# Gate and value projections of a gated MLP as seven half-width products per pair of chunks

## The chip, the cores and the metric

One NeuronCore of a Trainium2 chip runs the whole program in one launch. The metric is device time in microseconds of that launch. Three runs of the kernel before gave 1490.82 us as their median (1489.89 to 1491.82). A separate profiled execution took 1491.45 us; all rows of the trace shown here come from that one execution.

## The reference

A decoder trunk of two layers on 512 tokens of 1024 channels, in float32. Each layer has a token mixer (layer 0: a gated linear recurrence with pooling; layer 1: a Conformer convolution module), a cross-attention into 256 memory tokens, and a gated MLP. Only the MLP matters here:

```python
D_MODEL = 1024; SEQ = 512; D_FF = 3 * D_MODEL; CONV_F = 3

def conv_ffn(x, norm, w_up, dw_w, dw_b, w_down):
    h = rms_norm(x, norm) @ w_up                       # 1024 -> 6144
    g = causal_dwconv(h[..., :D_FF], dw_w, dw_b)       # gate half, 3 taps over tokens
    u = h[..., D_FF:]                                  # value half
    return (jax.nn.gelu(g) * u) @ w_down               # 3072 -> 1024

def reference(...):
    for layer in range(2):
        x = x + (mixer_ab if layer == 0 else conformer_conv)(...)
        x = x + cross_attn(x, mem, ...)
        x = x + conv_ffn(x, f_norm[layer], f_w_up[layer], ...)
    return rms_norm(x, final_norm)
```

## The kernel before

Activations lie with channels on the 128 partitions and the 512 tokens in the free dimension: `X[c]`, c from 0 to 7, each 128x512. A weight comes from HBM as a 128x1024 piece (512 KB) into a `raw` tile on the SP queue (`load_w`, L147). To keep float32 accuracy with the faster fp32r matmul, every operand is split in two: a high half, rounded by ACT (L161), and a low half, the difference, by DVE or, where told so, Pool (L162). `mm3` (L167 to L169) then makes three matmuls for each 128x128 weight block: high x high, high x low, low x high, all accumulated in one PSUM bank.

The MLP's 3072 gate and 3072 value channels are 24 chunks of 128 each. `up(c)` makes one gate chunk (eight weight blocks against eight activation tiles, 24 matmuls of 512 columns) and one value chunk. The activations it reads, `norm.x`, are X times the norm's gain, split but not yet divided by the root mean square; that scale, `norm.r`, is multiplied into the gate chunk on its way out of PSUM (L474) and into the result by Pool (L481). Between them stand the three taps (ACT L477, DVE L479 twice), the gelu (ACT L480), and the product with the value chunk out of PSUM (L483); the result is split into `ys[c]`. After every four chunks but the first four, `down(g)` multiplies the results of the group before with the down weights, eight products of 12 matmuls, each added to X by DVE (L494). The last group's down product goes together with the squares for the next norm (`nxt.feed`), or in layer 1 with the final norm (`finish`).

In layer 0 the memory tokens for layer 1's attention (`Memory(1)`) are loaded before the MLP and scaled and split (`mem.operand`, L312 and L313) in its second group. Four key weight pieces are split ahead ("parked") before the last down product.

A scheduler sets the order of instructions on each engine from dependencies and priorities: within `tc.high_priority(n)` instructions are drawn ahead. Tiles come from pools with a fixed number of buffers; a tile waits until a buffer is free. PSUM has five banks for products (`main_ps`), two further ones (`aux_ps`) and one for statistics.

Of the kernel before, what the change touches and what calls it, by code (L numbers as in the profile page):

```python
# [10 lines left out]
F32 = mybir.dt.float32  # L11
# [4 lines left out]
P = 128  # L16
# [12 lines left out]
AHEAD = 100  # L29
URGENT = 600  # L30
# [27 lines left out]
def trunk(ctx: ExitStack, tc: tile.TileContext, I: dict, out: list):  # L58
# [83 lines left out]
    def load_w(src=None, eng=None, raw=None, parts=1, ahead=AHEAD, park=False):  # L142

        with tc.high_priority(0 if raw is not None else ahead):
# [107 lines left out]
    def scale_of(ps, n=T, keep=False):  # L252
        sd = tmp_f(n)
        A.activation(sd, ps[:, :n], AF.Sqrt, bias=eps)
        r = small.tile([P, n], F32, tag="rs" if keep else "r", name=nm("r"), bufs=1 if keep else 2)
        V.reciprocal(r, sd)
        return r
# [209 lines left out]
    def ffn(layer, norm, nxt, mem=None):  # L467
        ys = {}

        def up(c):  # L470
            ps = project(load_w(I["wup"][(layer * 2) * CF + c]), c, norm.x)
            g = tmp_f(T + 2)
            G.memset(g[:, :2], 0.0)  # L473
            V.tensor_tensor(g[:, 2:], ps, norm.r, op=ALU.mult)  # L474
            y = tmp_f()
            dw = lambda j: col("f_dw_w", (layer * 3 + j) * CF + c)
            A.activation(y, g[:, 2:], AF.Identity, scale=dw(2), bias=col("f_dw_b", layer * CF + c))  # L477
            for j in (1, 0):
                V.scalar_tensor_tensor(y, g[:, j : j + T], dw(j), y, op0=ALU.mult, op1=ALU.add)  # L479
            A.activation(y, y, AF.Gelu_apprx_tanh)  # L480
            G.tensor_tensor(y, y, norm.r, op=ALU.mult)  # L481
            ps = project(load_w(I["wup"][(layer * 2 + 1) * CF + c]), c, norm.x)
            V.tensor_tensor(y, ps, y, op=ALU.mult)  # L483
            ys[c] = split(y)

        def down(g):
            for j in range(C // 2):
                w = load_w(I["wdown"][(layer * NG + g) * (C // 2) + j])
                for i in range(2):
                    n = 2 * j + i  # L490
                    ps = mm_ps()
                    for k in range(GC):
                        mm3(ps, blk(w, k * 2 * P + i * P), ys[g * GC + k], k == 0, k == GC - 1)
                    V.tensor_tensor(X[n], X[n], ps, op=ALU.add)  # L494
                    if g == NG - 1:
                        nxt.feed(n)

        for g in range(NG):
            for c in range(g * GC, (g + 1) * GC):
                up(c)  # L500
            if g:
# [533 lines left out]
```

## Time and profile before

| | |
|---|---|
| median of three runs | 1490.82 us |
| profiled execution | 1491.45 us |
| its span | 1489.6 us |
| MLP of layer 0 | about 365 to 757 us in the span |
| MLP of layer 1 | from about 1092 us to the end |
| DMA | 156.76 MB, 105 GB/s in the mean |

The columns of the views are these. In the list of groups: line, engine, operation, tile written <- tiles read, shapes, count, then total busy us and mean ns of one, then idle time of that engine just before them and what ended it. In a timeline: start us, duration us, engine, line, operation; "x4" behind it means four in a row merged into one entry. In the table of windows: stretch, its length, busy us (and count) of PE, PEld, DVE, ACT and POOL, granted clock, DMA share, GB/s. PE is the matmul engine, PEld its weight loads; `mm` and `aux` are PSUM tiles, `whi`, `wlo` and `act` split operands, `tmp` 128x512 work tiles, `bigr` 128x1024 split operands. Matmuls are pipelined: one lists 0.28 or 0.39 us, but the next starts earlier.

### The profile page before, as it was taken

To read this page: it belongs to the slowest core of one execution; us is meant where nothing else is said; L and a number is where in the kernel's file an instruction comes from. 1 tells how busy PE (TensorE), PEld (TensorE's weight loads), DVE (VectorE), ACT (ScalarE), POOL (GpSimd) and SP (SyncE) were. 2 spreads that over 40 slices of the span, in tenths; PEclk is the share of its full clock that TensorE was granted. 3 is DMA by queue.
4 is the path that set the end of the run, shared out by engine and by line. 5 is a ranking of instruction groups with operands and counts; after the bars stand their busy time and mean duration, and the time that the engine had idled before them with its cause. 6 is when DMAs were issued, how large, how long until landed. Compare 5 with 4: busy or idle time off the path is not lost.

```text
span 1489.6 us, 17802 instructions
## 1 busy us (share of the span) xinstructions
PE 1471.9 (99%) x6948; PEld 1211.3 (81%) x6948; DVE 912.9 (61%) x1220; ACT 638.3 (43%) x894; POOL 202.1 (14%) x228
## 2 busy tenths in 40 slices
PE   8999999999999999999999999999999999999997
PEld 7988788888888888888887666888888888888887
DVE  7877774647655545455666996666565554555455
ACT  7568743435432323323435346544443332323333
POOL 0012300000110101001006862300001010101001
PEclk9999999999999999999999999999999999999999
DMA  7522343213333333333416553321223333333321
GB/s 277 158 88 97 114 127 94 68 37 114 99 99 97 90 96 99 100 99 97 149 52 176 163 147 127 110 85 57 77 94 99 99 99 100 90 96 97 99 85 57
DMA packets 46820, 156.76 MB, mean 105 GB/s; under 512 B 5264, under 2 KB 6288, under 8 KB 46736
## 3 DMA queue, kind: packets, MB, share of 16 engines
q1 hardware_dynamic: 46448, 155.36, 33.6%
q8 instruction: 54, 0.88, 0.2%
q10 hardware_dynamic: 288, 0.27, 0.1%
q14 instruction: 30, 0.25, 0.0%
HBM read 145.13 MB, written 2.10 MB: 99 GB/s over the span
## 4 chain that ended last, share of the span: by engine, by line
PE 85%; issue 3%; DVE 2%; POOL 2%; ACT 1%; DMA 0%; POOLq 0%; DVEq 0%; ACTq 0%
PE mm L167 27%; PE mm L168 27%; PE mm L169 26%; PE aux L169 1%; PE aux L168 1%; PE aux L167 1%; PE aux L809 1%; POOL tmp L664 1%; DVE wlo L162 1%; POOL act L162 0%; PE aux L417 0%; DVE big L640 0%; ACT whi L161 0%; DMA raw<-in_wv 0%; DVE act L162 0%
## 5 line engine op out<-in xcount | busy, mean ns | idle before, releaser
L169 PE MATMUL mm<-act,wlo 128*128 128x512 f32 (+1 forms) x1797 | 697.5, 388 | 2.5 <-DVE wlo L162 2.5
L167 PE MATMUL mm<-act,whi 128*128 128x512 f32 (+1 forms) x1797 | 698.5, 389 | 0.0
L168 PE MATMUL mm<-act,whi 128*128 128x512 f32 (+1 forms) x1797 | 697.6, 388 | 0.4 <-DVE act L162 0.4
L161 ACT ACTIVATE whi<-raw 128x1024 fp32r<-128x1024 f32 x259 | 274.0, 1060 | 575.1 <-PE mm L168 477.4
L167 PEld LDWEIGHTS mm<-act,whi 128*128 128x128 f32 x1797 | 337.3, 188 | 73.9 <-issue 3.3
L169 PEld LDWEIGHTS mm<-act,wlo 128*128 128x128 f32 x1797 | 337.3, 188 | 72.0 <-DVE wlo L162 3.3
L168 PEld LDWEIGHTS mm<-act,whi 128*128 128x128 f32 x1797 | 337.4, 188 | 69.7 <-DVE act L162 1.3
L162 DVE TENSOR_TENSOR wlo<-raw,whi 128x1024 fp32r<-128x1024 f32 x239 | 296.5, 1242 | 65.3 <-ACT whi L161 62.5
L481 POOL TENSOR_TENSOR tmp<-tmp,r 128x512 f32<-128x512 f32 x48 | 62.0, 1292 | 637.5 <-ACT tmp L480 632.6
L494 DVE TENSOR_TENSOR x<-x,mm 128x512 f32<-128x512 f32 x88 | 60.4, 687 | 97.0 <-PE mm L169 97.0
L474 DVE TENSOR_TENSOR tmp<-mm,r 128x512 f32<-128x512 f32 x48 | 33.2, 692 | 125.7 <-PE mm L169 125.6
L483 DVE TENSOR_TENSOR tmp<-mm,tmp 128x512 f32<-128x512 f32 x48 | 33.2, 691 | 95.5 <-POOL tmp L473 87.2
L834 DVE SCALAR_TENSOR_TENSOR aux<-h,par,aux 128x491 f32<-128x491 f32 (+16 forms) x106 | 71.9, 726 | 2.1 <-PE aux L809 1.1
L479 DVE SCALAR_TENSOR_TENSOR tmp<-tmp,par,tmp 128x512 f32<-128x512 f32 x96 | 71.9, 749 | 1.7
L480 ACT ACTIVATE tmp<-tmp 128x512 f32<-128x512 f32 x48 | 30.4, 632 | 95.1 <-DVE tmp L479 95.1
L162 POOL TENSOR_TENSOR wlo<-raw,whi 128x1024 fp32r<-128x1024 f32 x20 | 49.1, 2464 | 124.6 <-ACT whi L161 124.5
L161 ACT ACTIVATE act<-tmp 128x512 fp32r<-128x512 f32 x84 | 52.6, 630 | 23.4 <-DVE tmp L676 7.1
L162 DVE TENSOR_TENSOR act<-tmp,act 128x512 fp32r<-128x512 f32 x84 | 59.8, 715 | 4.1 <-ACT act L161 4.0
L473 POOL MEMSET tmp<- 128x2 f32 x48 | 4.8, 100 | 298.2 <-DVE tmp L197 298.2
L477 ACT ACTIVATE tmp<-tmp,par 128x512 f32<-128x512 f32 x48 | 38.5, 803 | 0.6 <-DVE tmp L474 0.6
L832 POOL TENSOR_TENSOR actf<-actf,tmp 128x499 f32<-128x499 f32 (+7 forms) x28 | 36.4, 1299 | 11.5 <-ACT actf L828 10.2
L168 PE MATMUL aux<-act,whi 128*128 128x512 f32 x79 | 30.7, 389 | 0.0
(241 smaller groups left out, 1313.5 us busy)
## 6 DMA issues: line engine op xcount, KB each, us to landing
raw<-in_wup SPq DMA_DIRECT2D x96, 512.0 KB, 3.6
raw<-in_wdown SPq DMA_DIRECT2D x48, 512.0 KB, 3.5
raw<-in_pw SPq DMA_DIRECT2D x24, 512.0 KB, 4.0
raw<-in_win SPq DMA_DIRECT2D x20, 512.0 KB, 3.5
raw<-in_wv SPq DMA_DIRECT2D x16, 512.0 KB, 4.7
raw<-in_wk SPq DMA_DIRECT2D x16, 512.0 KB, 3.7
raw<-in_wq SPq DMA_DIRECT2D x16, 512.0 KB, 3.5
raw<-in_wo SPq DMA_DIRECT2D x16, 512.0 KB, 3.6
```

The costliest lines, as they stand in the source:

```text
L161: A.activation(hi, src, AF.Copy)
L162: (eng or V).tensor_tensor(lo, src, hi.bitcast(F32), op=ALU.subtract)
L167: PE.matmul(ps, wh, xh, start=first, stop=False)
L168: PE.matmul(ps, wh, xl, start=False, stop=False)
L169: PE.matmul(ps, wl, xh, start=False, stop=last)
L474: V.tensor_tensor(g[:, 2:], ps, norm.r, op=ALU.mult)
L477: A.activation(y, g[:, 2:], AF.Identity, scale=dw(2), bias=col("f_dw_b", layer * CF + c))
L479: V.scalar_tensor_tensor(y, g[:, j : j + T], dw(j), y, op0=ALU.mult, op1=ALU.add)
L481: G.tensor_tensor(y, y, norm.r, op=ALU.mult)
L494: V.tensor_tensor(X[n], X[n], ps, op=ALU.add)
L832: G.tensor_tensor(z[:, s:], z[:, s:], f[:, s:], op=ALU.add)
L834: V.scalar_tensor_tensor(ps[:, s:], h[:, : T - s], tap(s, c), ps[:, s:], op0=ALU.mult, op1=ALU.add)
```

## The change

The first four chunk pairs of each MLP keep the plain form. For the other 20, a gate and a value chunk are taken together as a 2x2 matrix of blocks: rows are gate and value, columns are the two halves of the 1024 input channels (512 each); the activations are a 2x2 matrix of input half by token half (256 tokens). A scheme of seven block products replaces the eight. Each product is 4 weight blocks x 3 matmuls of 256 columns.

- `Seven` holds seven operands made once per MLP from the scaled activations: three blocks B11, B21, B22 as they are and four combinations T1 to T4. Here the scale `norm.r` is multiplied in before the split, so these 20 pairs need no scaling later. It works in two halves of the channels (`operand(0)`, `operand(1)`).
- `Blocks` holds the weights of a pair: four 128x512 blocks of which a11 (in `r`) and the value block (in `z`) come in one load and a12, a22 in two. Their splits are a11, a12, a22 and four sums s1 to s4, formed in place: four DMAs on Pool's queue add one SBUF block into another, r += z after a11 is split, z += a22 after a22, r += a22 after s3, r += a12 after s2.
- `unit(c)` is one pair: seven products, in between seven weight splits for the pairs c to c + 2, seven additions of 128x256 that put the gate and value chunks together out of PSUM, the taps and gelu, and two of the eight down products of the group before (`Down`), each with its addition to X.
- `opening()` interleaves the eight plain products of the first four pairs with the making of the seven operands, the first pair's block splits and the second's first ones. Low halves of four operands and of the first pair's blocks are put on Pool.
- PE, ACT, DVE and Pool run the opening and the units in exactly the order written (`tc.manual_schedule`).
- In layer 0, loading and scaling the memory tokens moves behind the units.
- Small ones: one buffer in place of two for the scale tile, four in place of three for the `h` tiles (they also hold a12 and a22), and the weights are laid out anew on the host before the launch.

```diff
+ORDERED = {mybir.EngineType.PE, mybir.EngineType.Activation, mybir.EngineType.DVE, mybir.EngineType.Pool}
...
+    class Seven:
+        B11, B21, B22, T1, T2, T3, T4 = range(7)
...
+        def operand(self, h):
+            two = lambda t: t.rearrange("p (a b) -> p a b", a=2)
+            f = [big_f(), wp.tile([P, D], F32, tag="wlo", name=nm("scaled"))]
...
+                    V.scalar_tensor_tensor(
+                        f[k][:, i * T : (i + 1) * T], X[c], col(self.norm.gain[0], self.norm.gain[1] + c), self.norm.r,
+                        op0=ALU.mult, op1=ALU.mult,
+                    )
+            G.tensor_tensor(t3, b22, b12, op=ALU.subtract)
+            G.tensor_tensor(t1, b11, b12, op=ALU.subtract)
+            yield
+            part(self.B11, b11)
+            part(self.B21, b21)
+            part(self.B22, b22)
+            yield
+            V.scalar_tensor_tensor(t2, t3, -1.0, b11, op0=ALU.mult, op1=ALU.subtract)
+            V.scalar_tensor_tensor(t4, t2, -1.0, b21, op0=ALU.mult, op1=ALU.subtract)
+            part(self.T2, t2, G)
+            part(self.T3, t3, G)
+            yield
+            part(self.T1, t1, G)
+            part(self.T4, t4, G)
+
+        def product(self, ps, w, j):
+            for c in range(4):
+                at = slice(c * M, (c + 1) * M)
+                mm3(ps, blk(w, c * P), (self.x[j][0][:, at], self.x[j][1][:, at]), c == 0, c == 3)
+            return ps
...
+    class Blocks:
...
+        def part(self, name, eng=None):
...
+            self.w[name] = split(of, self.hi[:, at], self.lo[:, at], eng) if at else split(of, eng=eng)
+            if name == "a11":
+                G.dma_start(self.r, self.z, accum_op=ALU.add)
+            elif name == "a22":
+                G.dma_start(self.z, self.a22, accum_op=ALU.add)
+            elif name == "s3":
+                G.dma_start(self.r, self.a22, accum_op=ALU.add)
+            elif name == "s2":
+                G.dma_start(self.r, self.a12, accum_op=ALU.add)
...
+        def unit(c):
+            def m(j, block):
+                return seven.product(main_ps()[:, :M], pairs[c].w[block], j)
+            f, g, u, v = tmp_f(), tmp_f(), tmp_f(), tmp_f()
+            m1, u2, u3, u4 = u[:, :M], u[:, M:], v[:, :M], v[:, M:]
+            ps = m(seven.B11, "a11")
+            if c - 1 in last:
+                last.pop(c - 1)()
+            ahead(c, "s4")
...
+            A.activation(m1, ps, AF.Copy)
+            ps = m(seven.B21, "a12")
+            ahead(c + 1, "s3" if c == first else "s1")
+            add(g[:, :M], ps, m1)
+            ps = m(seven.T2, "s2")
+            ahead(c + 2, "a11")
+            add(u2, ps, m1)
+            ps = m(seven.T3, "s3")
+            ahead(c + 1, "s2")
+            add(u3, ps, u2)
+            downs[c].out(0, aux_ps())
+            downs[c + 1].split()
...
+            ps = m(seven.T1, "s1")
...
+            ahead(c + 2, "a12")
+            add(u4, ps, u2)
+            add(f[:, M:], ps, u3)
+            ps = m(seven.B22, "s4")
+            ahead(c + 2, "a22")
+            add(g[:, M:], ps, u4)
+            ps = m(seven.T4, "a22")
+            ahead(c + 2, "s3")
+            y = taps_of(c, g)
+            downs[c].out(1, aux_ps())
+            def rest():
+                add(f[:, :M], ps, u3)
+                V.scalar_tensor_tensor(y, f, -1.0, y, op0=ALU.mult, op1=ALU.mult)
+                ys[c] = split(y)
+            last[c] = rest
...
+        with tc.manual_schedule(engines=ORDERED):
+            opening()
+            for c in range(GC, CF):
+                unit(c)
+            last.pop(CF - 1)()
+        if nxt:
+            mem = Memory(1)
+            mem.operand(0)
+            mem.operand(1)
+            mem.outputs()
...
-    mem = Memory(1)
-    parked = ffn(0, n2, n3, mem=mem)
+    mem, parked = ffn(0, n2, n3)
```

In the opening a step reads like this (the fourth of eight; `start(i)` is a plain product, `fetch` a load with its high half, `low` the low half):

```diff
+            start(3)
+            fetch(5)
+            t = gate(1)
+            low(w[-1])
+            ahead(first, "s1", G)
+            next(t)
+            gelu(1, t)
+            next(steps)
```

237 lines of the change are left out of this document (193 added, 44 removed).

## The prediction

> **What bounds the kernel now.** I read the head of the profile page first, then the table of windows over the feed-forward parts, then PE's timeline there.
>
> ```profile
> span 1489.6 us, 17802 instructions
> PE 1471.9 (99%) x6948; PEld 1211.3 (81%) x6948; DVE 912.9 (61%) x1220; ACT 638.3 (43%) x894; POOL 202.1 (14%) x228
> 387.00:403.00 16.00, 16.00 (x72) 13.24 (x71) 8.27 (x10) 5.72 (x7) 2.55 (x4) 1.00 0.34 98
> 1156.00:1460.00 304.00, 304.00 (x1348) 252.28 (x1347) 157.75 (x187) 95.31 (x111) 23.91 (x34) 1.00 0.30 93
> ```
>
> A window row gives length, then busy time of PE, PEld, DVE, ACT and POOL, the clock and the DMA share. PE never rests in either feed-forward part, at full clock; DVE works half the time, ACT a third. A step there is worth its matmul time, as long as the others keep up. So the question is the pace of matmuls, not their listed length, since they overlap.
>
> ```profile
> 371.27 0.39 PE L167 MATMUL mm<-act,whi 128*128 128x512 f32 x1
> 384.87 0.39 PE L167 MATMUL mm<-act,whi 128*128 128x512 f32 x1
> 37.01 0.28 PE L167 MATMUL mm<-bigr,whi 128*128 128x256 f32 x1
> 38.93 0.28 PE L168 MATMUL mm<-bigr,whi 128*128 128x256 f32 x1
> ```
>
> Between the first two starts lie 60 matmuls of 512 columns: 13.60/60 = 0.227 us each. Between the last two lie 16 of 256 columns (the memory keys, a 128x128 weight block each, exactly the form of the new products): 1.92/16 = 0.120 us. Half the columns cost 53% of the time.
>
> **The unit, PE.** A gate and a value chunk cost 2 x 8 x 3 = 48 matmuls of 512 columns, 48 x 0.2267 = 10.88 us. Seven products of 4 x 3 matmuls of 256 columns cost 84 x 0.120 = 10.08 us. Twenty pairs in each of two layers: 40 x 0.80 = 32 us off PE. One eighth fewer columns gives only 7%, because the weight blocks are reloaded more often. The first four pairs keep their form, and a unit's two down products (24 x 0.2267 = 5.44 us) are the same work as before, so a unit is 15.52 us of PE against 16.32.
>
> **The unit, DVE and ACT.** Rows for their instructions:
>
> ```profile
> 376.62 0.69 DVE L474 TENSOR_TENSOR tmp<-mm,r 128x512 f32<-128x512 f32 x1
> 377.23 1.22 DVE L162 TENSOR_TENSOR wlo<-raw,whi 128x1024 fp32r<-128x1024 f32 x1
> 378.36 1.53 DVE L479 SCALAR_TENSOR_TENSOR tmp<-tmp,par,tmp 128x512 f32<-128x512 f32 x2
> 885.06 0.42 DVE L351 TENSOR_TENSOR tmp<-mm,r 128x256 f32<-128x256 f32 x1
> 885.40 0.73 DVE L834 SCALAR_TENSOR_TENSOR aux<-h,par,aux 128x491 f32<-128x491 f32 x1
> L161 ACT ACTIVATE whi<-raw 128x1024 fp32r<-128x1024 f32 x259 | 274.0, 1060 | 575.1 <-PE mm L168 477.4
> L161 ACT ACTIVATE act<-tmp 128x512 fp32r<-128x512 f32 x84 | 52.6, 630 | 23.4 <-DVE tmp L676 7.1
> L480 ACT ACTIVATE tmp<-tmp 128x512 f32<-128x512 f32 x48 | 30.4, 632 | 95.1 <-DVE tmp L479 95.1
> L477 ACT ACTIVATE tmp<-tmp,par 128x512 f32<-128x512 f32 x48 | 38.5, 803 | 0.6 <-DVE tmp L474 0.6
> ```
>
> Queued back to back, DVE starts the next instruction 0.61 us after one of 512 elements, 1.13 after one of 1024, 0.34 after one of 256; a scalar_tensor_tensor takes 0.66 to 0.78. A new unit has 8 low halves of 512 (seven weight blocks, one result), 1 of 1024, 7 adds of 256 out of PSUM, 3 scalar_tensor_tensor and 2 additions to X: 4.9 + 1.1 + 2.4 + 2.2 + 1.2 = 11.8 us queued, 13.3 with every listed duration in full, against 15.52 of PE. Before it was half of 16.3. ACT has 8 of 0.63, one of 1.06, 0.80, 0.63 and a small copy (0.4 at most by these rows): 7.9 us. Both fit, though DVE's cover shrinks to 2 to 4 us; five PSUM banks let it lag four products.
>
> **The unit, adding DMAs.** Four per unit on Pool's queue, 256 KB each, SBUF to SBUF. No queue of Pool's moves data in this profile. The order makes a loop: the first add (into r) reads z, so the add into z waits for it to land; s1 waits for that one; and DVE and ACT reach the next pair's a11, which releases its first add, only after this pair's s1. So a unit cannot be shorter than two landings plus the splits between them, 2L + about 2.5 us (two high and low halves, 2 x 1.3). Behind a late s1 stand, on DVE, the add of the second product and all that follows, on ACT the next high halves; PE follows when its five banks are full. It stays hidden while L is below (15.5 - 2.5)/2 = 6.5 us. Nearest rows:
>
> ```profile
> raw<-in_wup SPq DMA_DIRECT2D x96, 512.0 KB, 3.6
> actf<-h SPq DMA_DIRECT2D x32, 256.0 KB, 4.8
> last<-big SPq DMA_DIRECT2D x1, 256.0 KB, 2.0
> DMA to landing us min/median/max: 3.7/4.8/5.9
> ```
>
> The last row belongs to actf<-h: SBUF to SBUF, same size, four at once. Bounds 2.0 and, for a transfer that must also read its target and is described by Pool, 5.9 plus a second pass of the 256 KB (2.0 at most), 8. I take 5, near the row of the same size and route: hidden, but with 1.5 us in hand only. The Trainium skill, "DMA: Bandwidth & Descriptors", section "Anatomy of one DMA — SWDGE (gpsimd) path", fits a Pool-issued transfer with 2.0 us plus bytes over 436 GB/s, an estimate of 2.6 us here, without accumulation; by it the loop is far from binding. No run here shows that figure. Weight traffic from HBM is unchanged (1.5 MB a unit), at a DMA share of 0.30 to 0.34, so the adds have room.
>
> **The opening.** While PE does the eight plain products (8 x 24 x 0.2267 = 43.5 us, 44.0 with the two statistics matmuls), DVE, ACT and now Pool must scale and split seven operands in two halves, on top of four gates and the blocks of the first pair. Pool takes low halves, which would be free if it ran beside DVE. It does not:
>
> ```profile
> 945.07 10.86 POOL L162 TENSOR_TENSOR wlo<-raw,whi 128x1024 fp32r<-128x1024 f32 x4 [12.48 <-ACT whi L161]
> 950.78 2.90 DVE L197 TENSOR_TENSOR tmp<-tmp,tmp 128x512 f32<-128x512 f32 x1
> 953.60 2.88 DVE L189 SCALAR_TENSOR_TENSOR act<-x,par,act 128x512 fp32r<-128x512 f32 x1
> 956.41 0.68 DVE L197 TENSOR_TENSOR tmp<-tmp,tmp 128x512 f32<-128x512 f32 x1
> L481 POOL TENSOR_TENSOR tmp<-tmp,r 128x512 f32<-128x512 f32 x48 | 62.0, 1292 | 637.5 <-ACT tmp L480 632.6
> 373.23 3.35 DVE L256 RECIPROCAL r<-tmp 128x512 f32<-128x512 f32 x1 [0.78 <-ACT tmp L254]
> 364.67 0.39 PE L167 MATMUL mm<-act,whi 128*128 128x512 f32 x1
> ```
>
> Beside Pool, L197 takes 2.90 us; alone, 0.68. Both have two SBUF inputs, and they alternate whole instructions. L834, with one input in PSUM, ran at its usual 0.73 (885.40) in a stretch where Pool worked too. The Trainium skill, "SBUF — State Buffer", section "Who interferes with whom", says a DVE instruction with two SBUF inputs contends with a GpSimd instruction that reads SBUF and whichever is second blocks fully. The trace agrees, 2.90 against 0.68. By the full block the stall below is 12 us a layer; the rows let each DVE instruction begin some 0.15 us before Pool's ends (953.60 + 2.88 - 0.75 = 955.73, Pool's end 945.07 + 10.86 = 955.93), by which it is 9, and the time 1480 in place of 1486.
>
> The sum: the scale is there at 373.23 + 3.35 - 364.67 = 11.9 us into the part. After it Pool has 4 products gelu x r, 4 subtractions, 8 operand low halves and 3 block low halves: 19 x 1.29 = 24.5 us. DVE has, with two SBUF inputs, 6 of 1024 (6.8) and 31 of 512 (8 scalings, 6 operand halves, 4 combinations, 8 taps, 4 result halves, 1 block), 31 x 0.66 = 20.5. In alternation 11.9 + 24.5 + 27.3 = 63.7 us until the last of the first four results is split; DVE's 8 reads of PSUM can run beside Pool. PE needs that result in its first down product, after 44.0 + 4 x 1.44 + 9 x 0.227 = 51.8 us. It stands 11.9 us, partly earlier, for weights that DVE splits late. Bounds: 9 (the handovers, 19 x 0.15) and 17 (eight ACT steps of 0.63 between DVE steps exposed). I take 12 a layer, 24 in all.
>
> **The ends.** The last pair's result needs an addition of 256, a scalar_tensor_tensor, a high and a low half after the last X addition: 0.61 + 0.4 + 0.75 + 0.63 + 0.69 = 3.1 us, against 9 x 0.227 = 2.0 of cover: 1.1 us a layer. In layer 0 the memory load and its scaling move behind the units, into the last down products (96 x 0.227 = 21.8 us), where DVE was two thirds busy:
>
> ```profile
> 736.00:760.00 24.00, 24.00 (x119) 20.25 (x117) 16.14 (x21) 10.24 (x14) 0.00 (x0) 1.00 0.29 88
> L313 DVE SCALAR_TENSOR_TENSOR bigr<-big,par,bigr 128x256 fp32r<-128x256 f32 x16 | 6.9, 476 | 3.4 <-ACT bigr L312 3.4
> ```
>
> Eight of 0.48 are 3.8 us; that window leaves 7.9 free, but four parked key pieces move there too (8 x 0.61). About 1 us. Ends: 3 us, from 1 to 6. The SP queue issues the same loads in another order; the page shows landings of 3.6 us against a unit's 15, so I put nothing on it. The dropped memsets and gate scalings were off PE's path.
>
> **Sum.** Profiled execution 1491.45 us (span 1489.6 and 1.85 around it), 0.6 above the median of the runs, 1490.82. 1491.45 - 32 + 24 + 3 = 1486.5, less 0.6: 1486 us.
>
> **Rivals.**
> - Opening hidden: Pool and DVE rarely collide because one waits for ACT while the other works. Then DVE alone has 27.3 + 8 x 0.61 = 32.2 us after 11.9, done at 44, before PE needs it: 1490.8 - 32 + 3 = 1462. For it: DVE idles between dependent steps. Against: the four-fold stretched rows.
> - The adds bind: from L = 6.5 us on, each further microsecond costs 2 us a unit, 80 in all, at a fixed place: s1 waiting for the add into z. At L = 7.5 a unit is 17.5 us, slower than before: 1486 + 40 x 2 = 1566. For it: 5.9 already occurs in plain copies, and nothing shows accumulation. Against: the median 4.8.
> - DVE binds the unit: waits for ACT inside its fixed order (0.63 each) on top of 13.3 us; with four exposed, 15.8, 0.3 a unit: 1498.
> - The change doesn't save PE time: if 256 columns ran at 0.130, 84 x 0.130 = 10.9 and nothing would be gained: 1518. The keys' rows speak against it.
>
> **Chances.** A run of this kernel can tell about 0.2%, 3 us. Adds hidden and the opening serial: 0.60; its own range, by the bounds (opening 18 to 34, ends 1 to 6), is 1478 to 1499: 0.34 faster, 0.11 same, 0.15 slower. Opening hidden 0.17, faster. Adds bind 0.17, DVE binds or pace lost 0.06, slower. Faster 0.51, same 0.11, slower 0.38. The range 1461 to 1518 leaves out most of the adds' case and little else.
>
> **What would show it.** Products starting 0.120 us apart and units 15.5 us apart in the steady part; PE idle only around the first unit of each layer, waiting for DVE low halves and the last of the four results; two-input DVE rows of 1.5 to 2 us beside Pool in the opening and none in the units; adds landing in 4 to 6 us. Wrong if PE waits in every unit (the adds, or DVE above 15 of 15.5 us busy), or if PE passes the opening without a gap.

## The result, and the profile after

Before 1490.94 us (1489.89 to 1491.82), after 1499.97 us (1499.24 to 1500.75), four runs each: ratio 1.0061, 95% interval [1.0043, 1.0078]. The change is slower by 9 us, 0.6%; the forecast was 1486 us, faster. The profiled execution of after took 1499.24 us.

The head of the page after, then the table of windows (length; busy time of PE, PEld, DVE, ACT, POOL; clock; DMA share) for the first four-block unit and for sixteen later units:

```profile
span 1497.5 us, 21974 instructions
PE 1457.3 (97%) x8388; PEld 1260.8 (84%) x8388; DVE 1102.4 (74%) x1684; ACT 729.3 (49%) x1162; POOL 344.5 (23%) x336
418.10:440.60 22.50, 18.27 (x109) 15.94 (x108) 13.16 (x19) 10.07 (x18) 9.90 (x9) 0.92 0.52 129
473.50:722.50 249.00, 249.00 (x1730) 233.26 (x1729) 191.65 (x334) 111.89 (x189) 53.41 (x66) 1.00 0.73 166
```

PE works 14.6 us less, yet the span is 7.9 us longer: PE now waits. It doesn't wait in the steady units (249.00 of 249.00 busy, DVE 77%), but in the first one. PE's timeline at the first matmul of the first, second, third, fourth and last unit of layer 0:

```profile
418.02 0.28 PE L168 MATMUL mm<-bigr,whi 128*128 128x256 f32 x1
440.63 0.28 PE L168 MATMUL mm<-bigr,whi 128*128 128x256 f32 x1
457.97 0.28 PE L168 MATMUL mm<-bigr,whi 128*128 128x256 f32 x1
473.53 0.28 PE L168 MATMUL mm<-bigr,whi 128*128 128x256 f32 x1
722.49 0.28 PE L168 MATMUL mm<-bigr,whi 128*128 128x256 f32 x1
```

From the fourth to the last unit, (722.49 - 473.53)/16 = 15.56 us each. The first takes 22.61, the second 17.34, and the first begins 53.1 us into the part (which starts at 364.91), not 44.0. So the opening loses 9.1 + 7.05 + 1.8 = 17.9 us. In layer 1 the part starts at 1093.53 and its first unit at 1145.23, 51.7 us later; the first two units take 22.61 and 16.09, so the same count gives 7.7 + 7.05 + 0.53 = 15.3 us, 33.2 together. Against that stand 40 x (16.32 - 15.56) = 30.4 us gained in the units; the rest of the 7.9 us, about 5, lies elsewhere and is taken apart at the end of this section.

What PE waits for in the opening (timeline; in brackets idle time and what ended it), and two rows of DVE and Pool before that:

```profile
367.41 3.96 DVE L198 TENSOR_TENSOR tmp<-tmp,tmp 128x512 f32<-128x512 f32 x1
368.01 1.57 POOL L163 TENSOR_TENSOR wlo<-wa,whi 128x512 fp32r<-128x512 f32 x1
372.09 0.50 PE L229 MATMUL stat<-act,ones 128*128 128x512 f32 x1 [1.57 <-ACT act L162]
411.31 0.58 PE L170 MATMUL mm<-act,wlo 128*128 128x512 f32 x1 [3.12 <-DVE wlo L580]
411.69 0.63 PE L168 MATMUL mm<-act,whi 128*128 128x512 f32 x1
412.11 0.63 PE L169 MATMUL mm<-act,whi 128*128 128x512 f32 x1
431.52 0.50 PE L169 MATMUL aux<-act,whi 128*128 128x512 f32 x1 [1.14 <-DVE act L163]
432.09 0.41 PE L168 MATMUL mm<-bigr,act 128*128 128x256 f32 x1
432.30 0.42 PE L169 MATMUL mm<-bigr,act 128*128 128x256 f32 x1
```

An addition that takes 0.68 us alone takes 3.96 beside Pool. Low halves of weights (411.31) and the fourth result (431.52) come late, as forecast. New is the pace behind the gaps: 512-column matmuls stand 0.42 us apart instead of 0.227, 256-column ones 0.21 instead of 0.120. And a second wait follows the opening, with the adding DMA behind it: ACT waits, behind it DVE, and behind DVE PE in the second unit.

```profile
439.77 0.63 ACT L162 ACTIVATE act<-raw 128x512 fp32r<-128x512 f32 x1 [7.07 <-DMA raw<-wa]
445.21 0.35 PE L168 MATMUL mm<-bigr,act 128*128 128x256 f32 x1 [1.55 <-DVE tmp L610]
```

The remainder is 7.9 + 30.4 - 33.2 = 5.1 us. Points that the traces before and after share split it: the ends of the two feed-forward parts cost 1.3 us in layer 0 and 0.6 in layer 1, and 0.2 us stands ahead of layer 0's part. The other 3 us lie some 160 us behind layer 0's last unit, in the mixer of layer 1, which the change does not touch. There PE waits longer for ACT, whose instruction stands behind the splits of value weights that land late (SP's queue and PE, after and then before; `raw<-in_wv` are these weights, `wa<-in_wpair` a block of layer 1's first pair):

```profile
890.68 0.33 SPq L531 DMA_DIRECT2D wa<-in_wpair  x1
891.11 11.43 SPq L148 DMA_DIRECT2D raw<-in_wv  x5
904.49 1.93 PE L240 MATMUL stat<-actf,onesf 128*32 128x512 f32 x8 [4.76 <-ACT actf L1146]
883.08 11.57 SPq L147 DMA_DIRECT2D raw<-in_wv  x5
898.02 1.07 PE L239 MATMUL stat<-actf,onesf 128*32 128x512 f32 x8 [2.23 <-ACT actf L845]
```

The stage itself runs 4.2 us later than before (PE at 884.68 for 880.44), but these loads are issued 8.0 us later, behind loads for layer 1's first pair on the same queue, and the matmuls behind the wait run at a granted clock of 0.50. The wait is 4.5 to 5.8 us in every experiment too. That the order of the loads is the cause is read from the traces; no run moved them.

### The profile page after: what moved, and what is told of

The parts are those of the page before. It is cut to its first block, busy times and chain, and to the rows that moved or that the text cites. A ratio compares the mean times of both kernels' runs of the same rounds, so it can differ in the third digit from the quotient of the medians.

```text
span 1497.5 us, 21974 instructions
## 1 busy us (share of the span) xinstructions
PE 1457.3 (97%) x8388; PEld 1260.8 (84%) x8388; DVE 1102.4 (74%) x1684; ACT 729.3 (49%) x1162; POOL 344.5 (23%) x336
## 3 DMA queue, kind: packets, MB, share of 16 engines
q0 software_dynamic: 23040, 41.95, 16.7%
## 4 chain that ended last, share of the span: by engine, by line
PE 74%; DVE 7%; issue 5%; DMA 3%; ACT 3%; POOL 2%; SPq 0%; ACTq 0%; POOLq 0%; DVEq 0%
PE mm L168 18%; PE mm L170 18%; PE mm L169 18%; PE aux L168 6%; PE aux L169 6%; PE aux L170 6%; PE aux L1110 1%; DVE tmp L565 1%; DVE wlo L163 1%; DVE wlo L580 1%; DVE act L163 1%; DMA raw<-wa 1%; POOL tmp L701 1%; DMA big<-in_wdown 1%; ACT whi L162 1%
## 5 line engine op out<-in xcount | busy, mean ns | idle before, releaser
L170 PE MATMUL mm<-act,wlo 128*128 128x512 f32 (+1 forms) x829 | 323.4, 390 | 8.8 <-DVE wlo L580 6.2
L168 PE MATMUL mm<-act,whi 128*128 128x512 f32 (+1 forms) x829 | 323.6, 392 | 0.5 <-ACT act L162 0.5
L169 PE MATMUL mm<-act,whi 128*128 128x512 f32 (+1 forms) x829 | 323.1, 390 | 0.0
L168 PE MATMUL mm<-bigr,act 128*128 128x256 f32 x832 | 237.1, 285 | 2.2 <-DVE tmp L610 1.9
L162 ACT ACTIVATE whi<-raw 128x1024 fp32r<-128x1024 f32 (+1 forms) x161 | 152.0, 948 | 178.7 <-PE mm L169 94.9
L169 PE MATMUL mm<-bigr,act 128*128 128x256 f32 x832 | 237.1, 285 | 0.0
L170 PE MATMUL mm<-bigr,act 128*128 128x256 f32 x832 | 236.7, 284 | 0.0
L170 PEld LDWEIGHTS mm<-act,wlo 128*128 128x128 f32 x829 | 156.8, 189 | 42.6 <-DVE wlo L580 7.9
L168 PEld LDWEIGHTS mm<-act,whi 128*128 128x128 f32 x829 | 156.7, 189 | 37.8 <-issue 3.3
L163 DVE TENSOR_TENSOR wlo<-raw,whi 128x1024 fp32r<-128x1024 f32 (+1 forms) x139 | 152.5, 1102 | 43.6 <-ACT whi L162 41.5
L169 PEld LDWEIGHTS mm<-act,whi 128*128 128x128 f32 x829 | 156.8, 189 | 32.1 <-DVE act L163 1.3
L168 PEld LDWEIGHTS mm<-bigr,act 128*128 128x128 f32 x832 | 160.9, 193 | 4.6 <-issue 2.2
L169 PEld LDWEIGHTS mm<-bigr,act 128*128 128x128 f32 x832 | 161.0, 193 | 1.9 <-issue 0.2
L168 PE MATMUL aux<-act,whi 128*128 128x512 f32 x407 | 159.8, 393 | 2.6 <-ACT act L162 1.3
L170 PE MATMUL aux<-act,wlo 128*128 128x512 f32 x407 | 158.8, 390 | 3.3 <-DVE wlo L163 3.3
L169 PE MATMUL aux<-act,whi 128*128 128x512 f32 x407 | 159.6, 392 | 2.3 <-DVE act L163 2.3
L170 PEld LDWEIGHTS mm<-bigr,act 128*128 128x128 f32 x832 | 160.9, 193 | 0.2 <-issue 0.2
L163 POOL TENSOR_TENSOR wlo<-raw,whi 128x1024 fp32r<-128x1024 f32 (+1 forms) x22 | 51.8, 2366 | 415.2 <-ACT whi L162 415.1
```

Of the source, the lines that this page charges most:

```text
L162: A.activation(hi, src, AF.Copy)
L163: (eng or V).tensor_tensor(lo, src, hi.bitcast(F32), op=ALU.subtract)
L168: PE.matmul(ps, wh, xh, start=first, stop=False)
L169: PE.matmul(ps, wh, xl, start=False, stop=False)
L170: PE.matmul(ps, wl, xh, start=False, stop=last)
```

## The experiments

"Opening loss" is the time from the stat matmul's start (less its wait) to the third unit's start, less the 69.7 us that it takes without a stall, summed over both layers. The stall-free figure is 38.56 us from stat matmul to first unit, as the first run below showed, plus two units. By this measure the change loses 32.9 us, 0.3 less than by the count above, since a wait is listed from the modelled end of the matmul before it and not from the moment at which the next one could have started. "Before" was 1490.94 us beside the change and 1491.2 to 1491.4 us beside the experiments; e1, e4 and e9 were executed once each.

| kernel | us | ratio to before | opening loss, us |
|---|---|---|---|
| the change | 1499.97 | 1.0061 [1.0043, 1.0078] | 32.9 |
| e1 Pool writes only | 1472.18 | one run | 4.8 |
| e2 low halves on DVE | 1492.38 | 1.0008 [0.9999, 1.0018] | 26.7 |
| e3 all on DVE | 1494.39 | 1.0019 [1.0010, 1.0029] | 29.4 |
| e4 second add | 1546.28 | one run | not read |
| e5 scale first | 1500.68 | 1.0059 [1.0044, 1.0074] | 35.3 |
| e6 PSUM operands | 1495.00 | 1.0019 [1.0009, 1.0028] | 27.3 |
| e7 e2 + PSUM operands | 1495.43 | 1.0025 [1.0016, 1.0035] | 28.5 |
| e8 shared low halves + PSUM | 1494.01 | 1.0017 [1.0007, 1.0026] | 27.8 |
| e9 gaps filled | 1500.47 | one run | 33.1 |
| e10 e8 mended, second pair earlier | 1490.55 | 0.9993 [0.9984, 1.0002] | 24.1 |
| e11 second pair earlier | 1497.07 | 1.0038 [1.0025, 1.0052] | 30.8 |
| e12 e2 + second pair earlier | 1489.77 | 0.9986 [0.9977, 0.9995] | 22.7 |
| e13 first unit's gaps filled | 1501.72 | 1.0068 [1.0056, 1.0081] | 36.0 |
| e14 e12, fourth gate first | 1496.23 | 1.0036 [1.0022, 1.0050] | 29.5 |
| e15 e11, fourth gate first | 1503.36 | 1.0080 [1.0066, 1.0093] | 36.4 |
| e16 e14 mended | 1487.75 | 0.9975 [0.9965, 0.9985] | 21.8 |
| e17 e15 mended | 1494.74 | 1.0024 [1.0015, 1.0033] | 28.6 |

### Do Pool and VectorE take turns?

**e1: Pool only writes in the opening.** Each two-input operation of Pool there became two memsets; DVE's work is untouched.

```diff
-        (eng or V).tensor_tensor(lo, src, hi.bitcast(F32), op=ALU.subtract)
+        if eng is G and blank[0]:
+            G.memset(lo.bitcast(F32), 0.0)
+            G.memset(lo.bitcast(F32), 0.0)
...
-            G.tensor_tensor(t3, b22, b12, op=ALU.subtract)
+            blank_out(t3)
```

> Left out: in the two openings each of Pool's two-input instructions (low halves, subtractions, gelu x scale) is replaced by two memsets of its output, about as long, which read nothing from SBUF. Theory (DVE and Pool take turns whenever both read two SBUF operands or one): DVE's stretched rows return to about 0.7 us, DVE alone needs 32 us plus some 5 us of waits for ACT after the scale, the first unit starts about 46 to 48 us into the MLP (53.1 in the changed kernel) and the second 15.6 to 18 us after it (22.6): about 24 us less, 1474 to 1480. Rival (DVE's own amount of work and its waits for ACT in the fixed order set the opening): first unit at 52 to 53, second at 21 to 23 after it, 1496 to 1500.

PE at the first and second unit, and its one wait behind them; then the windows from the scale to the fourth result's low half, of the change and of e1 (columns as above):

```profile
409.00 0.28 PE L178 MATMUL mm<-bigr,whi 128*128 128x256 f32 x1
424.56 0.28 PE L178 MATMUL mm<-bigr,whi 128*128 128x256 f32 x1
429.67 0.36 PE L178 MATMUL mm<-bigr,act 128*128 128x256 f32 x1 [2.00 <-DVE tmp L620]
378.75:431.47 52.72, 45.43 (x210) 36.70 (x208) 45.22 (x47) 25.50 (x40) 33.02 (x23) 0.97 0.33 95
376.51:415.70 39.19, 39.19 (x198) 33.41 (x197) 32.53 (x47) 24.39 (x38) 20.66 (x40) 1.00 0.45 126
```

The first unit takes 15.56 us and starts on time; of the 32.9 us, 28.1 are gone, and the time is 27.8 us lower, a little below the theory's range. The same 47 instructions of DVE are busy 12.7 us less, and the fourth result is there 13.5 us sooner behind the scale. Two memsets take 1.05 us where a low half takes 1.29, and they wait for no high half, so Pool also has less to do here; but the shrinking of DVE's own rows shows the taking of turns as the main cause. What e1 leaves, 4.8 us, lies in the second units: waits of 2.00 and 0.74 us, and slower matmuls behind them (clock 0.91 in layer 0's second unit). The Trainium skill, "SBUF — State Buffer", section "Who interferes with whom", says that a GpSimd instruction that only writes SBUF does not contend with VectorE's two-input ones. This run agrees.

**e2: Pool's low halves on VectorE.**

```diff
-            part(self.T2, t2, G)
-            part(self.T3, t3, G)
+            part(self.T2, t2)
+            part(self.T3, t3)
...
-                ahead(first, name, G)
+                ahead(first, name)
```

> All low halves that the opening gives to Pool go to DVE (14 per layer, 11 of them after the scale); Pool keeps the subtractions and gelu x scale. Theory (taking turns): 11 times 1.29 us of Pool become 11 times 0.61 on DVE in the same serial sum, so the last of the first four results comes 5 to 8 us earlier in each layer: 1484 to 1490. Rival (DVE's own amount of work sets it): DVE gets 7 to 9 us more per layer and the time is 1510 or more.

7.6 us are back, less than expected. The window ahead of the first unit shows why:

```profile
400.00:412.70 12.70, 10.86 (x46) 8.67 (x47) 12.66 (x16) 5.68 (x10) 5.55 (x4) 1.00 0.38 105
```

DVE is busy 12.66 of 12.70 us. The low halves that left Pool are now volume on DVE, and that is the next bound, close behind the first. From the scale to the fourth result it takes 51.6 us, where the alternating sum would be about 45 (52.8 less 11 x 0.68); DVE is busy for 45.5 of them.

**e3: the subtractions and the multiplies by the scale on VectorE too.**

```diff
-            G.tensor_tensor(t3, b22, b12, op=ALU.subtract)
+            V.tensor_tensor(t3, b22, b12, op=ALU.subtract)
...
-                G.tensor_tensor(y[c], y[c], norm.r, op=ALU.mult)
+                V.tensor_tensor(y[c], y[c], norm.r, op=ALU.mult)
```

> As e2_lows_on_dve, and the four subtractions and four products gelu x scale go to DVE too; Pool only issues adding DMAs. Theory (taking turns): DVE has 44 us after the scale and nothing beside it, against 52.8 measured, so 8 to 10 us less per layer, and no DVE row of the opening is stretched: 1479 to 1484. Rival (DVE's amount of work): 1515 or more.

A miss: 2.0 us slower than e2, between the two ranges. No turns are left to take, but DVE got more work and now also stands behind GELU (2.04 us idle at 383.89 for ACT's L567); scale to fourth result still takes 52.1 us, DVE busy for 44.2. The Pool operations that e2 kept are worth having.

**e6: one SBUF input instead of two.** Same share on Pool; 16 DVE instructions a layer read PSUM.

```diff
-                g = tmp_f()
-                V.tensor_tensor(g, ps.pop(2 * c), norm.r, op=ALU.mult)
+                g = ps.pop(2 * c)
+                V.tensor_tensor(g, g, norm.r, op=ALU.mult)
...
+            norm.rp = aux_ps()
+            A.activation(norm.rp, norm.r, AF.Copy)
```

> The gate's product stays in its PSUM bank, and ScalarE copies the scale to a PSUM bank that the operand scalings read, so that 16 VectorE instructions a layer (8 of the multiplies ahead of GELU and the operand scalings of the opening) have one SBUF input instead of two. GpSimd's work is as in the changed kernel. Theory that a GpSimd operation waits for VectorE operations with two SBUF inputs and for no others: the contending VectorE work of an opening falls from 27.3 to about 17 us, the last first-pair result comes up to 10 us earlier, and the time is 1480 to 1488 us. Rival, that GpSimd is slowed by any VectorE work: no difference, 1500 us within 0.3%.

```profile
422.82 0.55 PE L168 MATMUL mm<-bigr,act 128*128 128x256 f32 x1 [5.02 <-DVE tmp L565]
```

The first unit starts 4 to 5 us sooner in each layer (413.22 instead of 418.02), with the same instructions on both engines. No scaling and no tap of its opening takes over 0.75 us, where the change has some of 1.6 to 1.8: two inputs in SBUF are what collides. But a product that stays in its PSUM bank until its taps are done made a wait of 5.0 us for that bank in each layer, and the first units take 23.1 and 22.8 us. The time, 1495.00 us, lies between the two ranges.

**e7 and e8: the same with VectorE's low halves, and with them shared out.** e7 is e2 with e6's edit; e8 leaves only T1's and T4's low halves on Pool.

> As the kernel with all low halves on VectorE (1492.4 us), with the gate's product left in PSUM and the scale copied to PSUM as well. Theory that two SBUF inputs are what costs: the 6 remaining GpSimd operations of an opening meet fewer rivals and VectorE loses less, 2 to 4 us a layer, 1484 to 1489 us. Rival, that VectorE's own volume and ScalarE's high halves set the opening once GpSimd is nearly free: no change, 1491 to 1494 us.

> Low halves of the first pair shared out: six on VectorE with the two sums T2 and T3, T1's and T4's and the two differences on GpSimd with the multiplies by the scale after GELU; gate's product and scale in PSUM. Theory that the opening is the longer of VectorE's volume and the alternating sum of GpSimd's and VectorE's two-SBUF-input work: both some 40 us behind the scale here, against 52.8 in the changed kernel, so about 10 us a layer come back, 1478 to 1486 us, less than the 1490.9 of the kernel before. Rival, that waits for ScalarE's high halves and the two adding DMAs set it: 1490 to 1495 us, as with the low halves on VectorE.

e7 lost 3 us against e2 and came out above both its ranges: with few collisions left, the bank wait (3.90 us, again for L565) seems to cost more than the edit saves. e8 fell in its rival's range, with the same wait (3.85 us). They show the price of a held bank, and nothing more on the taking of turns.

**e5: the scale computed ahead of the first low halves.**

```diff
-            for name in ("a11", "a12", "a22"):
-                ahead(first, name, G)
             norm.r = rstd(norm.ss)
             Norm.due = None
+            for name in ("a11", "a12", "a22"):
+                ahead(first, name, G)
```

> In the changed kernel, GpSimd's low halves of three weight blocks run beside the VectorE splits that feed the squared sum, so the scale is ready 13.75 us into the stage, the stat matmuls on TensorE wait 1.57 and 0.22 us, and the 512-column matmuls behind that gap start 0.425 us apart. Here the scale is computed ahead of those three splits. Theory that this late scale is a part of the loss: the wait of 1.8 us and about 1.6 us of half clock go, some 3 us a layer, less what the three low halves then cost behind it (they fall into the alternation, 3 x 1.3 us at most): between 1493 and 1498 us. Rival, that the time is set by the sum of GpSimd's and VectorE's two-input work wherever it stands: the last result comes as late as before, and the time is 1500 us within 0.2%.

The stat matmul no longer waits and the scale comes 2.5 us earlier, but no time is gained: the rival holds. The three low halves that ran ahead of the scale now stand behind it, in the same alternation. The late scale was not a cost of its own.

### Are the adding DMAs hidden?

**e4: the first add issued twice.**

```diff
                 G.dma_start(self.r, self.z, accum_op=ALU.add)
+                G.dma_start(self.r, self.z, accum_op=ALU.add)
```

> Changed: the first adding DMA of each pair is issued twice, so r holds one block too often. Theory (the loop through the adds bounds a unit by the landings in series plus 2.5 us; two landings of about 4.8 us are hidden): with three in series a unit takes 3 x 4.8 + 2.5 = 17 us or a little more in the steady part, 15.56 before, so 1550 to 1585, and ACT waits for an add in every unit. Rival (landings overlap with everything and are not in series): units stay at 15.6 and the time at 1500 to 1503.

PE at the first and the last unit of layer 0 in e4, one wait of ACT there, and landing times of the two kinds of adds (KB each, median us), first e4's, then those of the page after:

```profile
416.41 0.28 PE L168 MATMUL mm<-bigr,whi 128*128 128x256 f32 x1
750.49 0.28 PE L168 MATMUL mm<-bigr,whi 128*128 128x256 f32 x1
530.82 0.63 ACT L162 ACTIVATE act<-raw 128x512 fp32r<-128x512 f32 x1 [7.77 <-DMA raw<-raw]
raw<-wa POOLq DMA_DIRECT2D x120, 256.0 KB, 4.3
raw<-raw POOLq DMA_DIRECT2D x80, 256.0 KB, 3.6
raw<-wa POOLq DMA_DIRECT2D x120, 256.0 KB, 5.0
raw<-raw POOLq DMA_DIRECT2D x40, 256.0 KB, 4.4
```

(750.49 - 416.41)/19 = 17.6 us a unit, 17.1 without the first unit and 16.7 in layer 1, against 15.56; the units are uneven, from 15.56 to 20.8 us. ACT waits 6 to 9 us for the doubled add in most units, so a third landing in series does bind, and two stay under 15.56. The size of the loop is not confirmed: with e4's own medians the theory's sum is 2 x 3.6 + 4.3 + 2.5 = 14.0 us, which would have stayed hidden, and the time, 1546.28, is below its range. So more than 2.5 us stands between the landings, or Pool's queue, which waits for the first add before it issues anything else, plays a part; no run separates the two.

**e11: the second pair's first split and s3 earlier in the order.**

```diff
+            ahead(second, "a11")
             start(7)
             t = gate(3)
-            ahead(second, "a11")
...
+            ahead(second, "s3")
             values(3)
```

> The changed kernel with the second pair's first split and its sum s3 earlier, and nothing else. Theory that here the taking of turns still comes last in the first unit, and the adding DMAs only in the second: the first unit keeps its 22.6 us, the second falls from 17.3 and 16.1 to 15.6 us, 1 to 3 us together, 1497 to 1499 us. Rival, that the split ahead of the fourth gate delays VectorE where it is late already: the first unit is longer by as much, 1500 to 1502 us.

The second unit takes 15.56 us in both layers, and the time falls by 2.9 us. The same edit gave 2.6 us on e2:

> As the run with all low halves on VectorE (1492.4 us), with the second pair's first split and its sum s3 earlier. Theory as with the shared low halves: the second unit's waits of 1.93 and 0.38 us go and its clock comes back, 1 to 3 us together, 1489 to 1491 us. Rival, that VectorE's volume in the first unit sets it: 1492 to 1494 us.

and 3.5 on e8, together with SBUF for the last gate:

> As the run with the shared low halves (1494.0 us), with two edits: the last gate's product goes to SBUF again (in that run TensorE waited 3.85 us in the first four-block unit for its PSUM bank), and the second pair's first split and its sum s3 come earlier, ahead of the fourth gate and ahead of the last values, so that its chain of adding DMAs starts about 2 to 4 us sooner. Theory that, once the taking of turns is relieved, the second pair's adding DMAs are next (VectorE idle 5.13 us at 436.5 behind ScalarE's 6.92 us for the DMA, TensorE 0.57 and 1.99 us behind them): the bank wait and most of these go, 3 to 5 us a layer, 1484 to 1489 us, under the 1490.9 of the kernel before. Rival, that VectorE's volume in the first unit sets it: 1491 to 1494 us.

e12 met its theory. e10 removed both waits that it named, but its first units take 21.5 and 24.0 us, after 21.2 in both layers of e8, so it came out between its two ranges.

### The clock behind the gaps

**e9: throw-away matmuls in the two longest gaps.**

```diff
+            for _ in range(fill):
+                PE.matmul(ps, blk(w[1:], 0)[0], norm.x[0][0], start=True, stop=True)
```

> The changed kernel, with throw-away matmuls put into TensorE's two longest waits of each opening: seven of 512 columns ahead of the squared sum's (wait 1.57 us) and twelve ahead of the eighth product's (wait 3.1 us); their results are overwritten. Theory that the half clock after a gap follows from TensorE's idleness: the clock row is 1.00 in both places, the 512-column matmuls behind stand 0.227 apart instead of 0.425, and the first four-block unit starts about 1.6 us earlier in each layer. The time then falls by 0 to 3 us, to 1497 to 1500 us, as the unit's own waits for VectorE and ScalarE can take the gain back. Rival, that the clock is given for another reason (the first matmuls of a new stage, say): half clock stays, nothing starts earlier, 1500 us.

The rows that answer to 411.69 and 412.11 above, the first unit, the third:

```profile
411.92 0.40 PE L168 MATMUL mm<-act,whi 128*128 128x512 f32 x1
412.15 0.40 PE L169 MATMUL mm<-act,whi 128*128 128x512 f32 x1
416.74 0.28 PE L168 MATMUL mm<-bigr,whi 128*128 128x256 f32 x1
457.94 0.28 PE L168 MATMUL mm<-bigr,whi 128*128 128x256 f32 x1
```

The pace is 0.23 again and the first unit starts 1.3 us earlier; the third starts where it did (457.97). Idleness causes the half clock, and at this place it costs nothing, since DVE ends the later waits: the one execution took 1500.47 us.

**e13: the gaps inside the first unit filled.**

```diff
                 for k in range(GC):
+                    if fill and k in (0, 3):
+                        idle = stat_ps()
+                        for _ in range(10 if k == 0 else 9):
+                            PE.matmul(idle, ones, ys[0][0], start=True, stop=True)
```

> The changed kernel with throw-away matmuls in the first four-block unit of each layer, ahead of the two places of its first down product where TensorE waits (ten of 512 columns at 424.3, nine at 429.1); their results go to a PSUM bank that nothing reads. In the changed kernel 256-column matmuls stand 0.213 us apart instead of 0.120 from 432.09 on, until about 435, which is worth 1.4 us in each layer, behind the last wait and so on the path that sets the end. Theory: the spacing is 0.120 throughout, each first unit is 1.0 to 1.4 us shorter, 1497 to 1498 us. Rival, that the later start of the second unit is set by its adding DMAs in any case: the second unit grows by what the first loses, 1500 us within 0.1%.

```profile
432.25 0.28 PE L168 MATMUL mm<-bigr,act 128*128 128x256 f32 x1
432.36 0.28 PE L169 MATMUL mm<-bigr,act 128*128 128x256 f32 x1
445.00 0.38 PE L168 MATMUL mm<-bigr,act 128*128 128x256 f32 x1 [1.99 <-DVE tmp L614]
459.24 0.28 PE L168 MATMUL mm<-bigr,whi 128*128 128x256 f32 x1
```

The rival's mechanism holds, at a time just above its range: in layer 0 the first unit is 1.3 us shorter, the second 2.6 us longer. In both kernels ACT waits for an adding DMA of the second pair until nearly the same moment (439.77 in the change, 439.56 here). The sum is worse by 1.3 us since the half clock has moved: PE comes to the second unit earlier, waits longer there (0.4 and 1.99 us for 1.55), and the matmuls behind stand 0.21 us apart until 448.6, where those of the change stand 0.12 apart. So in the change as it stands the half clock, 1.4 us at this place too, lies beside another wait.

### Volume, or the order of the last steps?

**e14 and e15: the fourth gate, its taps and GELU ahead of the second half's sums,** on e12 and on e11.

```diff
-            next(steps)
-            values(2)
-            close(2)
-
-            ahead(second, "a11")
             start(7)
             t = gate(3)
+            next(steps)
             next(t)
-            downs[first].split()
             gelu(3, t)
+            values(2)
+            close(2)
+            downs[first].split()
+            ahead(second, "a11")
```

> As the run with all low halves on VectorE and the second pair earlier (1489.8 us), with the fourth gate, its taps and its GELU moved ahead of the second half's sums and the third values, and the down weights' split moved ahead of the second pair's first. TensorE's waits in that run's first unit (1.02, 2.35 and 0.22 us) are all in the first down product, which needs the fourth result; VectorE reached that gate at 418.6 though its product was there at about 407.5. Theory that the chain gate, taps, GELU, scale, values, split behind it is what remains of the loss: the result comes some 4 us earlier, the first unit falls from 22.9 and 24.2 to 18 to 20 us, 1480 to 1486 us. Rival, that VectorE's volume alone sets the moment (it was busy 12.66 of 12.70 us ahead of the unit), so that another operand is late instead: 1488 to 1491 us.

> The same order of the last steps, with GpSimd's share as in the changed kernel, and the second pair earlier (1497.1 us without the reordering). Theory that here the alternation of GpSimd and VectorE sets the last result whatever the order, since each operation of both counts once: 1495 to 1498 us. Rival, that the chain behind the fourth gate was late for its place in the order here too: 1489 to 1494 us.

Both were slower by 6 us, outside all their ranges, for a reason of my own making (e14, ACT, then PE):

```profile
427.29 0.63 ACT L162 ACTIVATE act<-raw 128x512 fp32r<-128x512 f32 x1 [4.92 <-DMA raw<-raw]
430.02 0.80 PE L168 MATMUL aux<-act,whi 128*128 128x512 f32 x1 [4.22 <-ACT act L162]
```

The second pair's first split came later than before, and its s3, still ahead of the third values, waited for the DMA with the fourth result queued behind it. With the split behind `gate(3)` and s3 behind `close(3)`:

> As the run with the fourth gate first and all low halves on VectorE (1496.2 us), with the second pair's first split moved up behind the fourth gate and its sum s3 moved down behind the fourth result. In that run ScalarE stood 4.92 us and VectorE 3.76 us at s3, which had to wait for an adding DMA issued at 423.3, with the third values of the fourth result queued behind it; that edit of mine hid what it was to show. Theory that the chain behind the fourth gate is what remains: the values are multiplied at about 424.5 in place of 428.6, TensorE's wait of 4.2 and 5.0 us in the first down product falls under 1.5, the first unit takes 18 to 21 us, the second 15.6 to 17.5, 1481 to 1488 us. Rival, VectorE's volume: 1488 to 1491 us, as with the second pair earlier alone (1489.8).

> The same order, with GpSimd's share as in the changed kernel (with the split of the second pair earlier alone 1497.1 us; with the unlucky order 1503.4). Theory that the alternation of GpSimd and VectorE sets the last result here whatever the order: 1495 to 1499 us. Rival, that the order was at fault in the change too: 1488 to 1494 us.

PE's waits in e16's first unit, with the starts of the first two units, and the window over the end of the opening:

```profile
412.94 0.28 PE L168 MATMUL mm<-bigr,whi 128*128 128x256 f32 x1
417.86 0.38 PE L168 MATMUL mm<-bigr,act 128*128 128x256 f32 x1 [1.17 <-ACT bigr L162]
421.24 0.58 PE L168 MATMUL mm<-bigr,act 128*128 128x256 f32 x1 [1.79 <-DVE tmp L705]
435.51 0.28 PE L168 MATMUL mm<-bigr,whi 128*128 128x256 f32 x1
400.00:435.50 35.50, 30.10 (x154) 25.56 (x155) 31.09 (x42) 16.65 (x28) 11.55 (x10) 0.90 0.47 117
```

The wait for the fourth result is gone, but operands and a bank are late in its place, and the unit takes 22.6 us, not the theory's 18 to 21. Its waits add up to only 3.3 of the 7.0 us above 15.56; most of the rest is pace, with a granted clock of 0.85 over the unit. DVE is busy 31.09 of 35.50 us, which points to volume more than order, but no run shows it apart from the clock. So 1487.75 us lies in the theory's range by luck: the first unit was not what it said. e16 is the fastest kernel here, 3.5 us under before, ratio 0.9975 [0.9965, 0.9985]; e12's interval overlaps it. With Pool's share as in the change the mended order gave 2.3 us (e17), a little more than its theory allowed, and the unlucky one cost 6.3: the alternation seems to set most of the loss there, the order some of it.

## Why the prediction was wrong

- **The unit on PE: right.** 15.56 us for 15.52; 30.4 us gained for 32. No wait of PE in the steady units, DVE at 77%, as forecast.
- **The adds: right that they are hidden.** 4.4 and 5.0 us for the assumed 5, and e4 opened the loop; but the 2.5 us between the landings do not account for e4's units, so the margin of 1.5 us is not confirmed. The 2.6 us that the Trainium skill's "DMA: Bandwidth & Descriptors", section "Anatomy of one DMA — SWDGE (gpsimd) path", would give is not what accumulating transfers took. What the step left out is the second pair, whose adds start late because the opening is late: 1.8 and 0.5 us.
- **The opening: the step that failed, by its size.** The mechanism was the right one (e1, and e6 for the two inputs), and the alternating sum from the scale to the fourth result is 431.5 - 378.7 = 52.8 us for 51.8, in layer 1 1158.7 - 1105.9 = 52.8 again. But 12 us a layer were 17.9 and 15.3. In layer 0: the fourth result 14.8 us late instead of 11.9, since Pool's first three low halves met the squared sum (3.96 us for 0.68) and the scale came at 13.8 us instead of 11.9; then 1.4 us of half clock behind the last wait, which the prediction did not have; then 1.8 us in the second unit. Together 18.0. In layer 1 the scale came at 12.4 us: 13.4 + 1.4 + 0.5 = 15.3. That the sum was met within 1 us is in part luck: e2 and e3 take 8 us out of it, and the interval stayed at 51.6 and 52.1 us, as DVE's volume and its waits for ACT lie close below. The other estimate in the prediction, 9 us a layer by the handover, was further off (its rows give 0.20 us a handover, not 0.15). The terms of the loss are not independent: e5, e9 and e13 each took one away and gained nothing, since another wait lay beside it. Sums of single causes tell where the time lies, not what an edit returns.
- **The ends, and a term put at nothing.** The remainder was 5.1 us, for 3. The ends themselves cost 1.3 and 0.6 us, less than forecast; the 3 us in layer 1's mixer are in no term. The prediction put nothing on the new order of the SP queue's loads, since a landing of 3.6 us is short against a unit of 15; it asked this for the units alone, and the place where the loads came late lies outside them.
- **The sum.** 1486.5 was forecast for the profiled execution, 1499.24 came: 1.6 from the unit, 9 from the opening, 2 from the ends and the later loads together. With gain and loss nearly equal, an error of a third in one term, the opening, was enough to turn the sign.
- **The rivals.** The opening did not hide; e1, which makes it hide, ran at 1472.18 us, above the 1462 forecast for that. Neither the adds nor DVE bound the units, and 256 columns kept their 0.120 us. The time fell into the likeliest case's mechanism but 1 us beyond its range of 1478 to 1499, whose upper bound of 34 us for the opening held while the unit and the remainder went a little the wrong way. The wide range, 1461 to 1518, holds the time; the direction was the wrong one.

## What to carry to other kernels

A start-up stage that is paid once per layer can eat what forty steady units save; cost it with the same care, engine by engine, and count each two-SBUF-input operation of Pool as time of VectorE's. When a stage has several late operands side by side, taking one wait away shows only the next: look for the volume on the busiest engine (DVE here) and for the clock behind the gaps before the order. A step that waits for a DMA must not stand in an engine's order ahead of work that others need. And compare the traces beyond the stage that was changed: loads drawn ahead for one stage can delay another's.

## What the runs showed of the hardware

TensorE's granted clock falls to half behind short gaps: after waits of 3.12 us (411.31) and, following several waits in a row, 1.14 us (431.52), matmuls stood 0.42 and 0.21 us apart for some 3.4 us, and e9 and e13 kept the full pace where they filled the gaps. No single length decides. In e12 a gap of 2.35 us in layer 0 was followed by full pace, one of 2.34 us at the same place of layer 1 by half:

```profile
427.13 0.50 PE L168 MATMUL aux<-act,whi 128*128 128x512 f32 x1 [2.35 <-ACT act L162]
428.43 0.28 PE L168 MATMUL mm<-bigr,act 128*128 128x256 f32 x1
428.55 0.28 PE L169 MATMUL mm<-bigr,act 128*128 128x256 f32 x1
...
1146.49 0.51 PE L168 MATMUL aux<-act,whi 128*128 128x512 f32 x1 [2.34 <-ACT act L162]
1148.23 0.41 PE L168 MATMUL mm<-bigr,act 128*128 128x256 f32 x1
1148.45 0.42 PE L169 MATMUL mm<-bigr,act 128*128 128x256 f32 x1
```

The Trainium skill, "TensorE: Matmul & The Clock Gate", section "Part 1: The HAM clock gate (the "warmup" mystery)", tells of a free-running window of activity of about 3.4 us. That fits two equal gaps with unequal results; that an idle stretch must be as long as the window does not fit these rows.
